# A hybrid decoder layer: the order written out by hand goes on behind attention over ten branch tiles, with the first block sums of h inside it

## The chip, the cores and the metric

The kernel runs on one core of a Trainium2 chip. The metric is the device time of one execution in microseconds, lower is better. Times are medians over several executions. TensorE (PE) does the matmuls, VectorE (DVE) and ScalarE (ACT) the elementwise work and the reading of PSUM, SyncE (SP) issues the DMAs.

## The reference

One layer of width 1024 over 1024 positions in float32 (cut):

```python
h = rms_norm(x, norm_mix_pre)
q, k, v, cb, cc, cx, g_att, g_conv = split(h @ w_in)
y_att  = stick_breaking_attention(heads(q), heads(k), heads(v)) @ w_att_branch
y_conv = (cb * causal_dwconv(cc * cx, conv_mix_w)) @ w_conv_branch
merged = sigmoid(g_att) * y_att + sigmoid(g_conv) * y_conv
x = x + rms_norm(merged @ w_out, norm_mix_post)
h = rms_norm(x, norm_ffn_pre)
a, g = split(causal_dwconv(h @ w_up, conv_ffn_w))
x = x + rms_norm((gelu(g) * a) @ w_down, norm_ffn_post)
```

The attention has 8 heads of 64 and is strictly causal; both branches are 512 wide. The change touches the two branch products (`w_conv_branch`, short wc, and `w_att_branch`, short wa), the gates' weights, and sums of blocks of h.

## The kernel before

Each float32 operand is held as a high and a low half in float16, and every product is three passes: high by high, high by low, low by high. A weight is fetched, its squares are summed on ScalarE (`sumsq`, L57) and over the partitions by a matmul with one column (tile `pr`, L83, from a small cast `rb` on VectorE, L74 or L76). From the sum come a scale and its inverse (L90 to L93), and with the scale ScalarE writes the high half (L100, L199) and VectorE the low half (L101, L204).

**Attention.** It stands under `manual_schedule`: the engines get their rows in the order in which the program writes them. Between the units of attention a generator gives out fill tiles: projections, the conv products, the first gates, and the first four tiles of the conv branch (`branch(0, d)`, named wc0 to wc3). One fill step is three matmuls of 128 by 512. A table `steps` holds what else is issued at which fill step. `plan_weight` enters the stages of a weight there: fetch 56 steps ahead of its use, squares 46, total 40, the pr matmul 26, the high half 24 and the low half 20. `plan_p` does the same for the conv branch's input p, whose four pieces are split four steps apart.

**Behind attention** the order is set by the scheduler of Tile. There stand the conv tiles wc4 to wc7, the attention tiles wa0 to wa5 (24 matmuls each, two halves of 12 with a bank of PSUM each), and the gates. A half is read out with its scale `sgn` by ScalarE (conv, L498) or by VectorE (attention, L500), and its squares are summed on ScalarE. The weights wa0 to wa3 come from `prep`, which fetches and splits them in the order of a fixed sequence; each serves two tiles.

**Block sums.** The gates g1 to g7 are products by a scheme of seven block products in place of eight (`Pair`, `Gates`). It needs sums and differences of blocks of h. `blocks(q)` forms them for the two pairs of 128-row blocks, q = 0 and 1, on VectorE, each row over 128 by 1024: T1 (three rows, L689 to L693), T2 from T1, T4 from T2 (two rows each) and T3 (three rows). `halves` splits each (high on ScalarE, L679, low on VectorE, L680): T1, T2 and T3 into the three parts of hB, T4 over a part of hT. The gate weight has sums of its own (`pair_sums`) and four splits (`pair_split`). The products of a gate (L1093) follow as pg1a, pg1b, pg1c and so on; the pr of the next gate weight, g2, stands between pg1a and pg1b.

Of the kernel before, what the change touches and what calls it, by code (L numbers as in the profile page):

```python
# [38 lines left out]
class Layer:  # L39
# [278 lines left out]
    def mixer(self, mid):  # L318
        tc, nc, a = self.tc, self.nc, self.a
        hT = self.hp.tile([P, 2, KD, T], F16, tag="hT", name="hT")  # L320
        with ExitStack() as ph1:
# [157 lines left out]
            def branch(bi, d, pm):  # L479

                which = ("wc", "wa")[bi]
                name = f"{which}{d // 2}"
                w, inv = self.wdone[name] if bi == 0 else self.prep(name)
                sc = sgn[:, 4 * bi + d // 2:4 * bi + d // 2 + 1]
                if d % 2 == 0:
                    self.mul(sc, inv_x[bi], inv)
                y = self.slot([P, T], F32, f"y{which}{d}")
                for c in range(2):
                    ps = pm.tile([P, NH], F32, tag="pm", name=f"py{which}{d}_{c}")
                    n = 0  # L490
                    for k in range(4):
                        for wi, hi in PASSES:
                            nc.tensor.matmul(ps, w[0][:, wi, ds((d % 2) * NH + k * P, P)],  # L493
                                             acts[bi][k][:, hi, ds(c * NH, NH)], start=n == 0, stop=n == 11)
                            n += 1
                        yield
                    if bi == 0:
                        nc.scalar.activation(y[:, ds(c * NH, NH)], ps, AF.Copy, scale=sc)  # L498
                    else:
                        nc.vector.tensor_scalar(y[:, ds(c * NH, NH)], ps, sc, None, ALU.mult)  # L500
                self.sumsq(y, smy[:, 8 * bi + d:8 * bi + d + 1], f"y{which}{d}")
                ys[which, d] = y
# [105 lines left out]
            steps, n_fill = {}, 0  # L608
            for g, n, names in fill:
# [49 lines left out]
            with tc.manual_schedule(engines=ENGINES):  # L659
# [13 lines left out]
        m16 = []  # L673
        with ExitStack() as ph2:
            hB = self.h7p.tile([P, 2, 3, KH, NH], F16, tag="hB", name="hB")
            t4s = []

            def halves(dst, src):
                nc.scalar.activation(dst[:, 0], src, AF.Copy)  # L679
                nc.vector.tensor_tensor(dst[:, 1], src, dst[:, 0], ALU.subtract)  # L680

            def blocks(q):
                lo, hi = ds(0, NH), ds(NH, NH)
                kA, kB = ds(2 * q, 2), ds(KH + 2 * q, 2)

                def diff(name, p, m, hT_m=True):

                    t = self.slot([P, 2, NH], F32, f"{name}_{q}")
                    nc.vector.tensor_tensor(t, hT[:, 0, p[0], p[1]], hT[:, 0, m[0], m[1]] if hT_m else m,  # L689
                                            ALU.subtract)  # L690
                    nc.vector.tensor_tensor(t, t, hT[:, 1, p[0], p[1]], ALU.add)
                    if hT_m:
                        nc.vector.tensor_tensor(t, t, hT[:, 1, m[0], m[1]], ALU.subtract)  # L693
                    return t
                t1 = diff("T1", (kA, hi), (kA, lo))
                halves(hB[:, :, 0, ds(2 * q, 2), :], t1)
                t2 = diff("T2", (kB, hi), t1, False)
                halves(hB[:, :, 1, ds(2 * q, 2), :], t2)
                t4s.append(diff("T4", (kB, lo), t2, False))
                t3 = diff("T3", (kB, hi), (kA, hi))  # L700
                halves(hB[:, :, 2, ds(2 * q, 2), :], t3)

            def branches(*ds_):
                for d in ds_:
                    for _ in branch(1, d, pm):
                        pass

            def merge_m(d):
                for which, yw in (("gc", "wc"), ("ga", "wa")):
# [4 lines left out]
                return m
# [508 lines left out]
```

## Time and profile before

| | |
|---|---|
| median of 3 runs | 1371.24 us (1370.97 to 1372.31) |
| profiled execution, its own time | 1372.84 us |
| its span | 1371.1 us |
| mean granted clock of TensorE | 0.984 |
| TensorE busy | 1294.1 us, 94% |
| VectorE busy | 1004.2 us, 73% |
| ScalarE busy | 802.0 us, 58% |
| first matmul of wc4 | 406.90 us |
| first matmul of pg1a | 478.21 us |
| first matmul of pg3a | 533.46 us |

The last three rows are read from TensorE's timeline, in microseconds from the span's start. In the profile, L493 is a line of the program, and names are shown without their numbers: pywc is any conv tile, pywa any attention tile, T any of T1 to T4. An idle time is that of an engine just before a row, with what ended it. The granted clock is a share of full speed.

### The profile page before, as it was taken

To read this page: it belongs to the slowest core of one execution; us is meant where nothing else is said; L and a number is where in the kernel's file an instruction comes from. 1 tells how busy PE (TensorE), PEld (TensorE's weight loads), DVE (VectorE), ACT (ScalarE), POOL (GpSimd) and SP (SyncE) were. 2 spreads that over 40 slices of the span, in tenths; PEclk is the share of its full clock that TensorE was granted. 3 is DMA by queue.
4 is the path that set the end of the run, shared out by engine and by line. 5 is a ranking of instruction groups with operands and counts; after the bars stand their busy time and mean duration, and the time that the engine had idled before them with its cause. 6 is when DMAs were issued, how large, how long until landed. Compare 5 with 4: busy or idle time off the path is not lost. (4 is left out here: it accounts for less than half of the span.)

```text
span 1371.1 us, 16955 instructions
## 1 busy us (share of the span) xinstructions
PE 1294.1 (94%) x6543; PEld 592.0 (43%) x6543; DVE 1004.2 (73%) x1649; ACT 802.0 (58%) x1138; POOL 48.1 (4%) x69
## 2 busy tenths in 40 slices
PE   5999999999888789999999999999999999999997
PEld 2444434444333334444444444444444444444443
DVE  5478788787742988877898958945972892698748
ACT  6366565656565365665565666755764764576422
POOL 1000000000000000000110000010001001000001
PEclk9999999999999899999999999999999999999999
DMA  6034444445341112241421143265137228612115
GB/s 262 1 75 100 99 100 101 100 93 108 73 108 32 31 62 77 77 183 33 154 99 51 37 169 138 62 139 145 55 107 156 91 77 208 191 60 95 62 62 199
DMA packets 109392, 139.58 MB, mean 102 GB/s; under 512 B 79088, under 2 KB 79088, under 8 KB 109312
## 3 DMA queue, kind: packets, MB, share of 16 engines
q1 hardware_dynamic: 105360, 124.28, 30.3%
q0 software_dynamic: 3952, 14.23, 5.7%
q8 instruction: 51, 0.84, 0.2%
q14 instruction: 29, 0.24, 0.1%
HBM read 94.45 MB, written 25.17 MB: 87 GB/s over the span
## 5 line engine op out<-in xcount | busy, mean ns | idle before, releaser
L1093 PEld LDWEIGHTS <-wh_u 128*128 128x128 f16 x1848 | 178.8, 98 | 217.9 <-issue 4.1
L988 PE MATMUL pd<-wdh,f 128*128 128x512 f16 x1056 | 235.6, 385 | 10.1 <-DVE wdh L101 5.6
L988 PEld LDWEIGHTS <-f 128*128 128x128 f16 x1056 | 104.5, 99 | 139.8 <-issue 16.4
L1093 PEld LDWEIGHTS <-wh_g 128*128 128x128 f16 x588 | 57.1, 98 | 74.4 <-ACT jk_ywa L57 4.7
L803 PE MATMUL py<-wh_wo,m 128*128 128x512 f16 x384 | 83.9, 379 | 0.0
L100 ACT ACTIVATE wh_u<-ws_u,sc 128x1024 f16<-128x1024 f32 (+1 forms) x66 | 64.2, 998 | 25.6 <-DVE ws_u L928 13.1
L101 DVE SCALAR_TENSOR_TENSOR wh_u<-ws_u,sc,wh_u 128x1024 f16<-128x1024 f32 (+1 forms) x66 | 72.2, 1100 | 7.7 <-ACT wh_u L100 7.7
L992 ACT ACTIVATE y<-pd,sd 128x512 f32<-128x512 f32 x64 | 42.0, 693 | 60.5 <-PE pd L988 54.1
L542 DVE TENSOR_TENSOR_SCAN R<-R,zero 128x256 f32<-128x256 f32 (+3 forms) x64 | 49.2, 811 | 29.0 <-ACT R L529 28.9
L90 DVE TENSOR_SCALAR sc<-pr 128x1 int32<-128x1 int32 x75 | 10.9, 151 | 73.1 <-PE pr L83 73.1
L1170 DVE SCALAR_TENSOR_TENSOR ugu<-cgu,cw_g,ugu 128x1023 f32<-128x1023 f32 (+1 forms) x44 | 56.3, 1279 | 10.3 <-ACT ugu L1168 10.2
L1170 DVE SCALAR_TENSOR_TENSOR ua<-cau,cw_a,ua 128x1023 f32<-128x1023 f32 (+1 forms) x44 | 56.2, 1278 | 1.9 <-ACT ua L1168 1.8
L803 PEld LDWEIGHTS <-m 128*128 128x128 f16 x384 | 37.5, 98 | 44.1
L493 PE MATMUL pywa<-o,wh_wa 128*128 128x512 f16 x192 | 49.1, 420 | 1.9 <-ACT wh_wa L100 1.9
L529 ACT ACTIVATE R<-z,cz 128x1024 f32<-128x1024 f32 (+3 forms) x48 | 42.9, 894 | 13.0 <-PE z L525 8.1
L250 PE MATMUL pcc<-hT,wh_cc 128*128 128x512 f16 x192 | 44.4, 386 | 5.1 <-DVE k L407 5.1
L493 PE MATMUL pywc<-p,wh_wc 128*128 128x512 f16 x192 | 42.8, 379 | 6.4 <-ACT ywc L498 3.8
L354 PE MATMUL pv<-wh_v,hT 128*128 128x512 f16 x192 | 44.4, 382 | 4.0 <-DVE r_pre L217 1.7
L57 ACT ACTIVATE jk_u<-ws_u 128x1024 bf16<-128x1024 f32 x44 | 46.4, 1055 | 2.6 <-DMA ws_u<-w_up_nt 1.9
L561 DVE TENSOR_TENSOR R<-be,R 128x1024 f16<-128x1024 f32 (+3 forms) x48 | 45.3, 944 | 2.3 <-ACT R L559 2.0
L250 PE MATMUL pq<-hT,wh_q 128*128 128x512 f16 x192 | 43.8, 379 | 2.1 <-ACT hT L239 1.2
L551 DVE TENSOR_TENSOR be<-be,R 128x1024 f32<-128x1024 f32 (+3 forms) x48 | 45.7, 952 | 0.1
(610 smaller groups left out, 2523.8 us busy)
## 6 DMA issues: line engine op xcount, KB each, us to landing
ws_u<-w_up_nt SPq DMA_DIRECT2D x44, 512.0 KB, 3.5
yd<-y POOLq DMA_DIRECT2D x24, 512.0 KB, 5.3
ds<-w_down SPq DMA_DIRECT2D x22, 512.0 KB, 6.2
wd<-w_down SPq DMA_DIRECT2D x22, 512.0 KB, 3.5
ws_g<-w_in_nt SPq DMA_DIRECT2D x14, 512.0 KB, 3.5
x<-x SPq DMA_DIRECT2D x8, 512.0 KB, 8.6
ws_wo<-w_out SPq DMA_DIRECT2D x8, 512.0 KB, 6.6
xr<-x SPq DMA_DIRECT2D x8, 512.0 KB, 4.0
```

Source lines behind the costliest of these rows:

```text
L57: self.nc.scalar.activation(self.junk(f"jk_{name}"), src, AF.Square, accum_out=acc)
L100: self.nc.scalar.activation(dst[:, 0, :], src, AF.Copy, scale=s)
L101: self.nc.vector.scalar_tensor_tensor(dst[:, 1, :], src, s, dst[:, 0, :], ALU.mult, ALU.subtract)
L250: nc.tensor.matmul(ps, w[:, wi, ds(k * P, P)], hT[:, hi, k, ds(c * NH, NH)], start=n == 0, stop=n == last)
L493: nc.tensor.matmul(ps, w[0][:, wi, ds((d % 2) * NH + k * P, P)], acts[bi][k][:, hi, ds(c * NH, NH)], start=n == 0, stop=n == 11)
L542: nc.vector.tensor_tensor_scan(rev, rev, self.zero.broadcast_to([P, W]), 2.0 ** 14 if u["top"] else carry[tl][:, h, :], ALU.mult, ALU.add)
L551: nc.vector.tensor_tensor(t["be"][:, :, :W], t["be"][:, :, :W], t["R"][:, :, 1:W + 1], ALU.mult)
L561: nc.vector.tensor_tensor(wv[1], be[:, :, :W], wv[0], ALU.subtract)
L803: nc.tensor.matmul(ps, m16[k][:, hi, ds(tt * P, P)], wo[k][:, wi, sl], start=k == 0 and p == 0, stop=k == 7 and p == 2)
L988: nc.tensor.matmul(ps, f16[g][k][:, hi, ds(tt * P, P)], w[k][:, wi, sl], start=n == 0, stop=n == 3 * GROUPS[g] - 1)
L1093: nc.tensor.matmul(ps, w[wt][:, wi, ds(wc * NH + k * P, P)], self.block(i, hi, k), start=first and n == 0, stop=n == 3 * KH - 1, skip_grou ...
L1170: nc.vector.scalar_tensor_tensor(u[:, lag:], c[:, :T - lag], sm[:, 2 - lag:3 - lag], u[:, lag:], ALU.mult, ALU.add)
```

## The change

The written order goes on over ten more tiles, wc4 to wc7 and wa0 to wa5, at eight fill steps each. In its table now stand: the gate weight g1 with all stages (`plan_pair`, from step 22 of the new stretch on), the block sums T1 and T2 with their halves (`plan_blocks`, from steps 2 and 20 on), the first gating and merging. `plan_weight` now plans wc2, wc3 and wa0 to wa3, 16 steps apart, and `prep` isn't called for them. T3 and T4 come behind the stretch (`late_blocks`), T4 in place in T2's buffer. The first half of an attention tile is read out by ScalarE, the second by VectorE as before. The pieces of p are split three steps apart in place of four. No matmul and no DMA is added or taken away; eight reads of PSUM move from VectorE to ScalarE.

```diff
-                for f, q in [(total, 3), (across, 13), (power, 14)] + [(part(j), 15 + 4 * j) for j in range(4)]:
+                for f, q in [(total, 3), (across, 13), (power, 14)] + [(part(j), 15 + 3 * j) for j in range(4)]:
...
-                w, inv = self.wdone[name] if bi == 0 else self.prep(name)
+                w, inv = self.wdone[name]
...
-                    if bi == 0:
+                    if bi == 0 or c == 0:
                         nc.scalar.activation(y[:, ds(c * NH, NH)], ps, AF.Copy, scale=sc)
...
-            for e in (2, 3):
-                self.plan_weight(steps, f"wc{e}", n_fill + 16 * (e - 2))
+            for e in range(6):
+                self.plan_weight(steps, ("wc2", "wc3", "wa0", "wa1", "wa2", "wa3")[e], n_fill + 16 * e)
...
+            def plan_blocks(steps, q, at):
...
+                for f, g in ((lambda: sub(new("T1"), hT[:, 0, kA, hi_], hT[:, 0, kA, lo_]), 0),
+                             (lambda: add(t["T1"], t["T1"], hT[:, 1, kA, hi_]), 2),
+                             (lambda: sub(t["T1"], t["T1"], hT[:, 1, kA, lo_]), 4),
+                             (lambda: high(b1, t["T1"]), 6),
+                             (lambda: sub(new("T2"), hT[:, 0, kB, hi_], t["T1"]), 6),
+                             (lambda: low(b1, t["T1"]), 8),
+                             (lambda: add(t["T2"], t["T2"], hT[:, 1, kB, hi_]), 10),
+                             (lambda: high(b2, t["T2"]), 12),
+                             (lambda: low(b2, t["T2"]), 14)):
+                    steps.setdefault(at + g, []).append(f)
...
+            def late_blocks(q, t):
...
+                t3, t4 = self.slot([P, 2, NH], F32, f"T3_{q}"), t["T2"]
+                sub(t3, hT[:, 0, kB, hi_], hT[:, 0, kA, hi_])
+                add(t3, t3, hT[:, 1, kB, hi_])
+                sub(t3, t3, hT[:, 1, kA, hi_])
+                b3, b4 = hB[:, :, 2, ds(2 * q, 2), :], hT[:, :, kA, hi_]
+                high(b3, t3)
+                sub(t4, hT[:, 0, kB, lo_], t4)
+                low(b3, t3)
+                add(t4, t4, hT[:, 1, kB, lo_])
+                high(b4, t4)
+                low(b4, t4)
...
+                plan = [(fetch, 0), (lambda: squares(0), 10), (lambda: squares(1), 12), (done, 12), (total, 17),
+                        (lambda: self.pair_sums(n), 22), (across, 30), (power, 31)]
+                plan += [(lambda i=i, e=e: part(i, e), 32 + 4 * i + 3 * e) for i in range(4) for e in range(2)]
...
-            for d in range(4, 8):
-                for _ in branch(0, d, pm):
-                    pass
-            branches(0)
-            ms = [merge_m(0)]
-            branches(1, 2)
-            self.pair_fetch("g1")
...
+            later = [(branch(0, d, pm), 8) for d in range(4, 8)] + [(branch(1, d, pm), 8) for d in range(6)]
+            tq = [plan_blocks(steps, q, n_fill + 2 + 18 * q) for q in range(2)]
+            plan_pair(steps, "g1", n_fill + 22)
+            steps.setdefault(n_fill + 3, []).append(lambda: gated("gc", "wc"))
+            steps.setdefault(n_fill + 45, []).append(lambda: gated("ga", "wa"))
+            steps.setdefault(n_fill + 47, []).append(merged)
+            with tc.manual_schedule(engines=ENGINES):
+                for g, n in later:
+                    for _ in range(n):
+                        for f in steps.pop(state["done"], ()):
+                            f()
+                        next(g)
+                        state["done"] += 1
+                    next(g, None)
+            self.pair_fetch("g2")
             for q in range(2):
-                blocks(q)
-            branches(3)
-            for q in range(2):
-                halves(hT[:, :, ds(2 * q, 2), NH:], t4s[q])
-            self.pair_sums("g1")
-            self.pair_split("g1")
-            self.pair_fetch("g2")
-            branches(4, 5)
+                late_blocks(q, tq[q])
             self.pair_sums("g2")
```

How the rows stand on VectorE behind the last weight split of the conv branch, wh_wc3, before (rb, pr and sc of the sums of wa0 to wa2, wh_wa0 the low half of the first attention weight):

```order
L204 SCALAR_TENSOR_TENSOR wh_wc3_3777<-ws_wc3_3564,sc27_3681,wh_wc3_3777 128x1024
L76 CAST rb29_3986<-sm_wa0_3980 128x1
L90 TENSOR_SCALAR sc28_3985<-pr29_3988 128x1
L92 TENSOR_SCALAR sc28_3985<-sc28_3985 128x1
L93 TENSOR_SCALAR sc28_3985<-sc28_3985 128x1
L104 TENSOR_TENSOR sgn_446<-cst_438,sc28_3985 128x1
L76 CAST rb30_4047<-sm_wa1_3996 128x1
L101 SCALAR_TENSOR_TENSOR wh_wa0_0_3993<-ws_wa0_0_3981,sc28_3985,wh_wa0_0_3993 128x1024
L76 CAST rb31_4058<-sm_wa2_4001 128x1
```

and now, in the same place (T1_0 and T2_0 are the block sums of the first pair):

```order
L680 TENSOR_TENSOR T1_0_3878<-hT_104 128x1024
L794 TENSOR_TENSOR ywc0_3641<-ywc0_3641,sgc0_3361 128x1024
L683 TENSOR_TENSOR T1_0_3878<-T1_0_3878,hT_104 128x1024
L680 TENSOR_TENSOR T1_0_3878<-T1_0_3878,hT_104 128x1024
L90 TENSOR_SCALAR sc28_3784<-pr29_3896 128x1
L92 TENSOR_SCALAR sc28_3784<-sc28_3784 128x1
L93 TENSOR_SCALAR sc28_3784<-sc28_3784 128x1
L76 CAST rb30_3914<-sm_wa1_3787 128x1
L680 TENSOR_TENSOR T2_0_3920<-hT_104,T1_0_3878 128x1024
L680 TENSOR_TENSOR hB_3864<-T1_0_3878,hB_3864 128x1024
L204 SCALAR_TENSOR_TENSOR wh_wa0_3911<-ws_wa0_3685,sc28_3784,wh_wa0_3911 128x1024
L683 TENSOR_TENSOR T2_0_3920<-T2_0_3920,hT_104 128x1024
```

Block rows stand between the small rows of the sums, and the cast of wa0's sum stands ahead of this piece. Further on in the stretch the two rows of T4, written into T2's buffer, stand among them as well, for both pairs.

On TensorE the pr of wa0 (pr29) stood between the last conv tile, wc7, and the first attention tile, and that of wa1 inside it:

```order
L493 MATMUL pywc7_1_3964<-p16_3_3577,wh_wc3_3777 128x512
L83 LDWEIGHTS ones_85
L83 MATMUL pr29_3988<-rb29_3986,ones_85 128x1
L493 LDWEIGHTS wh_wa0_0_3993
L493 MATMUL pywa0_0_4013<-o16_0_993,wh_wa0_0_3993 128x512
```

Now the pr of wa0 stands in the second half of tile wc4:

```order
L493 MATMUL pywc4_1_3889<-p16_1_3509,wh_wc2_3679 128x512
L83 LDWEIGHTS ones_85
L83 MATMUL pr29_3896<-rb29_3785,ones_85 128x1
L493 LDWEIGHTS wh_wc2_3679
L493 MATMUL pywc4_1_3889<-p16_2_3541,wh_wc2_3679 128x512
```

In the same way those of wa1 and wa2 now stand in wc6 and wa0, and those of g1 and wa3 in wa2.

On VectorE ahead of the cast of g2's sum (rb34), which TensorE needs between pg1a and pg1b, stood before the read-out of wa5, one row of T3 and splits of g1:

```order
L500 TENSOR_SCALAR ywa5_4293<-pywa5_0_4294,sgn_446 128x512
L500 TENSOR_SCALAR ywa5_4293<-pywa5_1_4308,sgn_446 128x512
L73 TENSOR_REDUCE sc33_4344<-sm_g2_4252 128x1
L693 TENSOR_TENSOR T3_1_4185<-T3_1_4185,hT_104 128x1024
L928 TENSOR_TENSOR ws_g1_0_4143<-ws_g1_0_4143,s12_g1_4226 128x512
L101 SCALAR_TENSOR_TENSOR wh_g1_1_4240<-ws_g1_1_4147,sc32_4230,wh_g1_1_4240 128x1024
L74 CAST rb34_4345<-sc33_4344 128x1
```

and now:

```order
L500 TENSOR_SCALAR ywa5_4264<-pywa5_1_4279,sgn_446 128x512
L680 TENSOR_TENSOR T3_0_4305<-hT_104 128x1024
L683 TENSOR_TENSOR T3_0_4305<-T3_0_4305,hT_104 128x1024
L680 TENSOR_TENSOR T3_0_4305<-T3_0_4305,hT_104 128x1024
L680 TENSOR_TENSOR hT_104<-T2_0_3920,hT_104 128x2x512
L680 TENSOR_TENSOR T3_1_4315<-hT_104 128x1024
L680 TENSOR_TENSOR hB_3864<-T3_0_4305,hB_3864 128x1024
L683 TENSOR_TENSOR T3_1_4315<-T3_1_4315,hT_104 128x1024
L73 TENSOR_REDUCE sc33_4345<-sm_g2_4296 128x1
L104 TENSOR_TENSOR sc_g1_4417<-g_pre_122,sc31_4087 128x1
L991 TENSOR_TENSOR s12_g2_4325<-ws_g2_1_4301 128x512
L680 TENSOR_TENSOR T3_1_4315<-T3_1_4315,hT_104 128x1024
```

The cast of g2's sum is the row behind the last of these. The whole of T3 and a low half of T4, written to hT, now stand ahead of it, and the splits of g1 are done earlier.

More of the change, by code (lines that the diff above doesn't have):

```diff
@@ L663, in mixer @@
                 attention()
-            self.wpos = self.fpos = len(self.wseq) - 4
             pha.close()
@@ L675, in mixer @@
             hB = self.h7p.tile([P, 2, 3, KH, NH], F16, tag="hB", name="hB")
[L676 to L701, printed above, removed]
@@ new lines, in mixer, with k_of, sub, add @@
+            lo_, hi_ = ds(0, NH), ds(NH, NH)
+            def k_of(q):
+                return ds(2 * q, 2), ds(KH + 2 * q, 2)
+            def sub(out, x, y):
+                nc.vector.tensor_tensor(out, x, y, ALU.subtract)
+            def add(out, x, y):
+                nc.vector.tensor_tensor(out, x, y, ALU.add)
+            def high(dst, src):
+                nc.scalar.activation(dst[:, 0], src, AF.Copy)
+            def low(dst, src):
+                sub(dst[:, 1], src, dst[:, 0])
+            def plan_blocks(steps, q, at):
+                kA, kB = k_of(q)
+                t = {}
+                b1, b2 = [hB[:, :, e, ds(2 * q, 2), :] for e in range(2)]
+                def new(name):
+                    t[name] = self.slot([P, 2, NH], F32, f"{name}_{q}")
+                    return t[name]
+                for f, g in ((lambda: sub(new("T1"), hT[:, 0, kA, hi_], hT[:, 0, kA, lo_]), 0),
[8 more added lines that the diff above has]
+                    steps.setdefault(at + g, []).append(f)
+                return t
@@ new lines, in late_blocks @@
+            def late_blocks(q, t):
+                kA, kB = k_of(q)
+                t3, t4 = self.slot([P, 2, NH], F32, f"T3_{q}"), t["T2"]
[9 more added lines that the diff above has]
+                low(b4, t4)
@@ new lines, in plan_pair, with fetch, squares, done @@
+            def plan_pair(steps, n, at):
+                h = {}
+                def fetch():
+                    h["sm"] = self.small(f"sm_{n}", w=8)
+                    h["t"] = [self.ws.tile([P, D], F32, tag="ws", name=f"ws_{n}_{i}") for i in range(2)]
+                    for t, src in zip(h["t"], self.psrc[n]):
+                        nc.sync.dma_start(t, src)
+                def squares(i):
+                    self.sumsq(h["t"][i], h["sm"][:, i:i + 1], f"{n}_{i}")
+                def done():
+                    self.praw[n] = h["sm"], h["t"]
+                def total():
+                    h["r"] = self.scale_sum(h["sm"], 2)
+                def across():
+                    h["r"] = self.scale_mm(*h["r"])
+                def power():
+                    h["s"], h["inv"] = self.scale_pow(*h["r"], 1)
+                    h["w"] = [self.wh.tile([P, 2, D], F16, tag="wh", name=f"wh_{n}_{i}") for i in range(4)]
+                    self.pw[n] = h["w"], h["inv"]
+                def part(i, e):
+                    ua, ug, s12 = self.praw[n][1:]
+                    src = (ua, ug, s12, ua[:, hi_])[i]
+                    w = h["w"][i] if i < 3 else h["w"][3][:, :, :NH]
+                    if e == 0:
+                        nc.scalar.activation(w[:, 0], src, AF.Copy, scale=h["s"])
+                    else:
+                        nc.vector.scalar_tensor_tensor(w[:, 1], src, h["s"], w[:, 0], ALU.mult, ALU.subtract)
+                        if i == 0:
+                            sub(ua[:, hi_], ua[:, hi_], s12[:, hi_])
+                plan = [(fetch, 0), (lambda: squares(0), 10), (lambda: squares(1), 12), (done, 12), (total, 17),
+                        (lambda: self.pair_sums(n), 22), (across, 30), (power, 31)]
+                plan += [(lambda i=i, e=e: part(i, e), 32 + 4 * i + 3 * e) for i in range(4) for e in range(2)]
+                for f, g in plan:
+                    steps.setdefault(at + g, []).append(f)
@@ L720, in split_m, with gated, merged @@
                 m16.append(t)
-            for d in range(4, 8):
-                for _ in branch(0, d, pm):
-                    pass
-            branches(0)
-            ms = [merge_m(0)]
-            branches(1, 2)
-            self.pair_fetch("g1")
-            self.inv_h = inv_h
-            for q in range(2):
-                blocks(q)
-            branches(3)
-            for q in range(2):
-                halves(hT[:, :, ds(2 * q, 2), NH:], t4s[q])
-            self.pair_sums("g1")
-            self.pair_split("g1")
-            self.pair_fetch("g2")
-            branches(4, 5)
+            self.inv_h = inv_h
+            ms = []
+            def gated(which, yw):
+                y = ys[yw, 0]
+                nc.vector.tensor_tensor(y, y, sig[which, 0], ALU.mult)
+            def merged():
+                add(ys["wa", 0], ys["wa", 0], ys["wc", 0])
+                ms.append(ys["wa", 0])
+            later = [(branch(0, d, pm), 8) for d in range(4, 8)] + [(branch(1, d, pm), 8) for d in range(6)]
[12 more added lines that the diff above has]
+                    next(g, None)
+            assert not steps, sorted(steps)
+            self.pair_fetch("g2")
+            for q in range(2):
+                late_blocks(q, tq[q])
             self.pair_sums("g2")
```

## The prediction

> **What bounds the kernel now.** I read the busy times first, then a table of windows around the branch products, then TensorE's timeline there, the waits, and the lines that fill VectorE and ScalarE. The page's first part:
>
> ```profile
> PE 1294.1 (94%) x6543; PEld 592.0 (43%) x6543; DVE 1004.2 (73%) x1649; ACT 802.0 (58%) x1138; POOL 48.1 (4%) x69
> ```
>
> TensorE is the bound of the whole, so only its idle time and its slow clock can be won. Where they lie, by windows (start and end, length, busy time and count of PE, weight loads, DVE, ACT, POOL, then the granted clock, the DMA share and GB/s):
>
> ```profile
> 370.00:407.00 37.00, 30.27 (x193) 14.54 (x192) 20.62 (x34) 23.05 (x32) 0.00 (x0) 1.00 0.43 106
> 407.00:428.00 21.00, 20.78 (x96) 9.30 (x95) 0.00 (x0) 9.47 (x16) 0.00 (x0) 1.00 0.02 9
> 428.00:479.00 51.00, 36.85 (x153) 15.76 (x153) 42.81 (x64) 24.37 (x34) 0.00 (x0) 0.83 0.14 42
> 479.00:534.00 55.00, 49.81 (x220) 21.80 (x218) 44.52 (x72) 31.93 (x48) 0.00 (x0) 0.94 0.18 58
> 534.00:620.00 86.00, 86.00 (x405) 39.06 (x403) 70.18 (x117) 57.57 (x85) 1.13 (x2) 1.00 0.36 123
> ```
>
> From 407 to 428 (tiles wc4 to wc7) PE is full and VectorE does nothing at all for 21 us. From 428 to 479 VectorE is busy 42.81 of 51 us and PE waits for 14. After 534 PE is busy all the time, so what is won before is kept there. TensorE's timeline (start, duration, what, idle before and releaser):
>
> ```profile
> 382.96 0.16 PE L83 MATMUL pr<-rb,ones 128*128 128x1 bf16 x1 [0.32 <-ACT sga L477]
> 387.48 4.04 PE L493 MATMUL pywc<-p,wh_wc 128*128 128x512 f16 x18 [3.05 <-ACT ywc L498]
> 406.90 20.88 PE L493 MATMUL pywc<-p,wh_wc 128*128 128x512 f16 x96 [0.78 <-ACT ywc L498]
> 431.11 0.16 PE L83 MATMUL pr<-rb,ones 128*128 128x1 bf16 x1 [3.33 <-DVE rb L76]
> 433.14 1.89 PE L493 MATMUL pywa<-o,wh_wa 128*128 128x512 f16 x4 [1.87 <-ACT wh_wa L100]
> 464.99 0.16 PE L83 MATMUL pr<-rb,ones 128*128 128x1 bf16 x1 [9.17 <-DVE rb L74]
> 481.65 2.75 PE L1093 MATMUL pg1a<-hT,wh_g 128*128 128x512 f16 x12 [0.69 <-ACT cgg L1108]
> 488.81 0.16 PE L83 MATMUL pr<-rb,ones 128*128 128x1 bf16 x1 [4.41 <-DVE rb L74]
> 533.46 2.75 PE L1093 MATMUL pg3a<-hT,wh_g 128*128 128x512 f16 x12
> ```
>
> Every long stop stands ahead of a pr: the one-column matmul that sums a weight's squares over the partitions. It waits for the cast rb on VectorE; the waits of 428 to 515 add up to:
>
> ```profile
> DVE rb L76 <- ACT jk_wa L57: 26.4, 2, 26.2
> PE pr L83 <- DVE rb L74: 13.6, 2, 9.2
> PE pr L83 <- DVE rb L76: 3.3, 1, 3.3
> ```
>
> The first row is VectorE's empty time: its next row, the sum of wa0, waited 26.2 us for squares that came late. The block sums, which need only hT and were ready long before, stand behind it. The 9.17 us are the second effect: the sum of g1 stands on VectorE among the block sums. And a stop costs more than itself; the clock after two of them, and around 390 after the 3.05 us:
>
> ```profile
> 387.00:390.00 3.00, 2.52 (x12) 1.17 (x12) 1.55 (x6) 1.45 (x3) 0.00 (x0) 1.00 0.83 155
> 465.00:468.00 3.00, 3.00 (x9) 1.07 (x9) 3.00 (x4) 1.82 (x2) 0.00 (x0) 0.50 0.00 0
> 468.00:471.00 3.00, 3.00 (x9) 1.11 (x8) 3.00 (x6) 0.52 (x2) 0.00 (x0) 0.53 0.00 0
> 489.00:492.00 3.00, 3.00 (x8) 1.06 (x7) 3.00 (x3) 0.43 (x1) 0.00 (x0) 0.50 0.47 175
> 492.00:495.00 3.00, 3.00 (x9) 1.06 (x8) 2.94 (x9) 2.44 (x4) 0.00 (x0) 0.55 0.32 66
> ```
>
> A matmul takes 20.88 / 96 = 0.2175 us at full clock, so 6 us hold 27.6; after 9.17 us idle they held 18 and after 4.41 us 17. Such a stop costs 2.1 to 2.3 us beside itself; 3.05 us idle cost none.
>
> **The budget.** From 406.90 (first matmul of wc4) to 488.81 (pr of g2, between pg1a and pg1b) pass 81.9 us. They hold ten branch tiles and pg1a, 264 matmuls or 57.4 us at full clock; 3.33 + 1.87 + 9.17 + 0.69 + 4.41 = 19.5 us idle; and 5.0 us left over, which is the halved clock after the stops at 431 and 465 and the small rows.
>
> **The change part by part.** PE's work and order of tiles stay; ten tiles of 24 matmuls take 52.2 us, so without a stop wa5 ends at 406.9 + 52.2 = 459.1 in the clock of this trace (478.21 before, where pg1a begins). Whether it does depends on the hand-offs, which I walked through on all engines with these durations (the last number ahead of the bar is the count, the second behind it the mean in ns):
>
> ```profile
> L691 DVE TENSOR_TENSOR T<-T,hT 128x1024 f32<-128x1024 f32 x8 | 9.5, 1220 | 0.1
> L101 DVE SCALAR_TENSOR_TENSOR wh_wa<-ws_wa,sc,wh_wa 128x1024 f16<-128x1024 f32 x4 | 5.1, 1281 | 1.8 <-ACT wh_wa L100 1.8
> L500 DVE TENSOR_SCALAR ywa<-pywa,sgn 128x512 f32<-128x512 f32 x16 | 11.6, 744 | 2.4 <-PE pr L83 1.4 <-PE pywa L493 1.0
> L913 DVE TENSOR_TENSOR s_g<-ws_g 128x512 f32<-128x512 f32 x4 | 2.7, 681 | 0.0
> L498 ACT ACTIVATE ywc<-pywc,sgn 128x512 f32<-128x512 f32 x8 | 5.5, 687 | 11.4 <-PE pywc L493 11.4
> L57 ACT ACTIVATE jk_ywa<-ywa 128x1024 bf16<-128x1024 f32 x8 | 8.4, 1055 | 20.5 <-DVE ywa L500 16.1 <-DVE sc L90 4.4
> L679 ACT ACTIVATE hB<-T 128x1024 f16<-128x1024 f32 x6 | 6.3, 1049 | 3.7 <-DVE T L693 2.4 <-DVE T L691 1.2
> ```
>
> *Block sums and g1 ahead of wa.* VectorE is free from 404.7 (end of the last wc split, at 403.41 with 1.28). Up to the cast of g1's sum its new order holds 18 block rows and the gate of ywc0 at 1.22, two splits at 1.28 and 12 tiny rows at about 0.15: 27.6 us, which ends at 432.3 without gaps. Low parts wait for ScalarE's high parts of 1.05 us, and the scales of wa0 and wa1 for their pr; my walk puts 5.9 us for that, so the cast ends at 438.2. TensorE needs it after 156 matmuls, at 406.9 + 33.9 = 440.8: 2.6 us of room. For wa3 the walk gives 439.4 against 442.1, for the weights themselves 418.8 against 427.8 (wa0), 430.9 against 438.2 (wa1), 442.7 against 448.6 (wa2). In all, VectorE has 43 to 47 us of work in the 54.3 from 404.7 to 459, ScalarE about 41 in 51. So these moves cost nothing and take away the stops at 431, 433 and 465. Without that cover each pr costs its lateness one to one, and about 2.2 more once a stop passes some 3.5 us.
>
> *First halves evicted on ScalarE.* Eight rows of 0.744 us leave VectorE, eight of about 0.687 come to ScalarE. ScalarE is the emptier (9.47 of 21 us and 24.37 of 51); the cost is order: at the end of wa5 its row of pg1a (cgg) stands behind jk_ywa4, two rows of wa5 and the high part of T4. That puts it at 464.25, so the second half of pg1a starts 2.65 us late (0.69 before).
>
> *The block sums that stay late.* After wa5's last matmul VectorE must still do, ahead of g2's cast: the eviction (0.74), the three rows of T3 of the first pair, the low part into hT, a row of T3, the low part into hB, two more rows of T3 (8 x 1.22 = 9.76), one half sum of g2 (0.68) and three tiny rows (0.45). That is 11.6 us, and 0.4 for ScalarE's high part in between: 459.1 + 12.0 = 471.1. PE is done with pg1a at 464.25 + 2.75 = 467.0, so g2's pr stops it for 4.1 us. The pair pg1a and pr is thus as badly placed as before, only earlier: 471.1 for 488.81, a gain of **17.7 us**. Check by the budget: 57.4 + 2.65 + 4.1 = 64.2, 17.7 under 81.9.
>
> From there to pg3a it took 533.46 - 488.81 = 44.65 us, with the half clock of 489 to 495 in it. A stop of 4.1 follows too, so I leave that as it is, and the same holds for the weights of g2, whose DMA is fetched earlier by as much.
>
> *Closer splits of p, and wc2, wc3, wa0 planned in the table.* The stop at 387.48 hangs on VectorE's sgn, released late:
>
> ```profile
> 379.41 1.28 DVE L101 SCALAR_TENSOR_TENSOR p<-pf,sc,p 128x1024 f16<-128x1024 f32 x1 [2.70 <-ACT p L100]
> 380.61 1.28 DVE L204 SCALAR_TENSOR_TENSOR wh_wc<-ws_wc,sc,wh_wc 128x1024 f16<-128x1024 f32 x1
> 386.50 0.15 DVE L104 TENSOR_TENSOR sgn<-sc,sc 128x1 f32<-128x1 f32 x1
> 386.75 0.69 ACT L498 ACTIVATE ywc<-pywc,sgn 128x512 f32<-128x512 f32 x1 [2.81 <-DVE sgn L104]
> ```
>
> With the last part of p (1.28) ahead of it in a gap of 2.70, sgn comes about 1.2 us sooner and pywc at 387.48 with it. Against that, wa0's squares (1.05) and its 512 KB on SP now stand in the attention's tail, among the transposes: at worst the whole 1.2 is lost and 1.0 more. I take 1.2, since both engines idle there.
>
> **Sum.** 17.7 + 1.2 = 18.9 of the profiled execution's 1372.84: 1353.9. The median of the runs shown is 1371.24, 1.6 lower: **1352.3 us**.
>
> **A rule against the row.** The clock fell after idle of 4.41 us and not after 3.05. The Trainium skill, page "TensorE: Matmul & The Clock Gate", section "Part 1: The HAM clock gate (the "warmup" mystery)", gives a free-running window of about 3.4 us, and half clock until some 3.4 us of work have gone by. By that a stop costs 1.7 us in place of the 2.1 to 2.3 that the rows show, an estimate from its figure. As the window is free-running, a stop of 4.1 us need not fill one: by the page the time is the forecast or 1.7 less, 1350.6, depending on where the window falls, which no trace here shows.
>
> **The rivals.**
> *VectorE stays the limit, and the stops come back smaller (0.23).* For it: rooms of 2.6 and 2.7 us under 5.9 us of hand-offs that I could only estimate; the low parts pay a round trip through ScalarE each. If every one of some 25 crossings takes 0.3 us more than I gave it, 7.5 in all, the sums of g1 and wa3 come about 5 us after they are needed, with one stop at half clock on top: 5 + 2.2 = 7.2 less gain, about 1359. Against it: 428 to 479 shows VectorE keeping 42.81 of 51 us.
> *The last stop is not punished, or shorter (0.11).* If ScalarE reaches cgg in time, or T3 is put earlier by the engines' slack, the two stops shrink: 2.3 us of clock and up to 2.65 of pg1a: 1347 to 1349.
> *Slower (0.05).* Sums standing inside tiles hold matmuls that could run: PE takes its rows in order. If wa1, g1 and wa3 each wait as long as the two of L74 did (13.6 / 2 = 6.8, and 2.2 for the clock: 9 each, 27 together), the gain of 18.9 turns to 8 lost, 1379. It decides from a sum of 18.9 us of new stops on. Against it: each row of squares stands at least 18 fill steps of three matmuls (54 x 0.2175 = 11.7 us) ahead of its pr.
> *The gain is given back (0.03).* A transfer of g2 or g3 arrives no sooner than before and pg3a starts at 533 again: 1371. Fetches take 3.5 us and queues are nearly idle (0.14 and 0.18 in the windows):
>
> ```profile
> ws_g<-w_in_nt SPq DMA_DIRECT2D x14, 512.0 KB, 3.5
> ```
>
> **How the numbers follow.** The forecast has 0.58 and its own range, 1349.5 to 1355.5: the tail's term between -1.0 and 1.2, the late chain by one row of 1.22, the clock. The range is 1346 to 1360: the second rival whole and most of the first. A measurement of this kernel tells 0.2% (2.7 us) from no change. Faster: 0.58 + 0.23 + 0.11 = 0.92; same 0.03; slower 0.05.
>
> **What would show it.** VectorE is no longer empty while wc4 to wc7 run; the ten tiles take 52 to 53 us; no pr before pg1a waits over 1 us; a stop of about 4 us stays ahead of the pr between pg1a and pg1b, with about half clock behind it, and one of about 2.6 inside pg1a; the stop after pywc's first half is near 2 us in place of 3.05; after pg3a the two traces run alike. I am wrong if a pr inside wc4 to wa3 waits 3 us or more, or if the matmuls of the wa tiles run spread out.

## The result and the profile after

The changed kernel takes 1350.49 us (median, 1349.2 to 1353.69) against 1371.78 for the kernel before measured beside it: the ratio is 0.9843, 95% interval 0.9818 to 0.9868, so 1.6% or 21.3 us faster. The forecast was 1352.3 in a range of 1346 to 1360. The profiled execution took 1349.20 us.

TensorE's timeline of the changed kernel (start, duration, what, idle before and releaser):

```profile
382.92 0.16 PE L83 MATMUL pr<-rb,ones 128*128 128x1 bf16 x1 [1.43 <-ACT sga L477]
385.99 4.04 PE L493 MATMUL pywc<-p,wh_wc 128*128 128x512 f16 x18 [1.59 <-ACT ywc L498]
405.40 4.04 PE L493 MATMUL pywc<-p,wh_wc 128*128 128x512 f16 x18 [0.78 <-ACT ywc L498]
409.29 0.17 PE L83 MATMUL pr<-rb,ones 128*128 128x1 bf16 x1
419.67 0.17 PE L83 MATMUL pr<-rb,ones 128*128 128x1 bf16 x1
430.06 0.17 PE L83 MATMUL pr<-rb,ones 128*128 128x1 bf16 x1
439.15 0.17 PE L83 MATMUL pr<-rb,ones 128*128 128x1 bf16 x1
440.47 0.17 PE L83 MATMUL pr<-rb,ones 128*128 128x1 bf16 x1
457.33 2.75 PE L1171 MATMUL pg1a<-hT,wh_g 128*128 128x512 f16 x12
461.57 2.75 PE L1171 MATMUL pg1a<-hT,wh_g 128*128 128x512 f16 x12 [1.49 <-ACT cgg L1186]
468.78 0.16 PE L83 MATMUL pr<-rb,ones 128*128 128x1 bf16 x1 [4.46 <-DVE rb L74]
468.80 5.28 PE L1171 MATMUL pg1b<-hB,wh_g 128*128 128x512 f16 x12
513.17 2.75 PE L1171 MATMUL pg3a<-hT,wh_g 128*128 128x512 f16 x12
```

No pr between 405 and 457 has an idle time ahead of it any more, and the one between pg1a and pg1b has kept its own. By stage, from such rows of both kernels:

| stage | before, us | forecast, us | after, us |
|---|---|---|---|
| start to wc4 | 406.90 | 405.7 | 405.40 |
| wc4 to pg1a, the ten tiles | 71.31 | 52.2 | 51.93 |
| pg1a to the pr of g2 | 10.60 | 12.0 | 11.45 |
| that pr to pg3a | 44.65 | 44.65 | 44.39 |
| pg3a to the end of the profiled execution | 839.38 | 839.4 | 836.03 |

The ten tiles give 19.4 us, and up to pg3a the gain is 20.29 us in these two traces (18.9 forecast). The last row's 3.35 us is no part of the change. Behind pg3a the clock of the kernel before falls to half three times amid the work (at 798.5, 1126.1 and 1320.7 us), that of the changed kernel once (at 709.6), each time for 3.4 us, which costs about 1.7, so that two falls fewer make up the 3.35. In the twelve traces below this piece takes 833.97 to 838.93 us. The first row scatters as well: a second trace of the changed kernel reaches wc4 at 408.11 us. What the change did there is read from the stop, 3.05 us before and 1.59 after.

The windows of the changed kernel (columns as in the prediction):

```profile
402.00:428.00 26.00, 25.22 (x120) 11.36 (x118) 19.63 (x26) 17.52 (x26) 0.00 (x0) 1.00 0.14 42
428.00:459.00 31.00, 31.00 (x148) 14.07 (x146) 25.19 (x41) 21.32 (x34) 0.00 (x0) 1.00 0.25 82
459.00:469.00 10.00, 4.05 (x20) 1.69 (x18) 9.79 (x13) 9.67 (x16) 0.00 (x0) 0.92 0.03 10
469.00:513.20 44.20, 44.10 (x195) 19.39 (x194) 30.39 (x51) 20.83 (x29) 0.00 (x0) 0.94 0.16 48
```

VectorE, empty from 407 to 428 before, is now busy for 19.63 of the 26 us from 402 to 428, with TensorE at full clock. From 459 to 469 both VectorE and ScalarE are full and TensorE is not: that is where the block sums that stayed late stand. VectorE's rows at the places with the least room:

```profile
436.28 0.16 DVE L74 CAST rb<-sc 128x1 bf16<-128x1 f32 x1
437.32 0.15 DVE L76 CAST rb<-sm_wa 128x1 bf16<-128x1 f32 x1
439.41 1.28 DVE L204 SCALAR_TENSOR_TENSOR wh_wa<-ws_wa,sc,wh_wa 128x1024 f16<-128x1024 f32 x1 [1.94 <-ACT wh_wa L199]
457.53 0.75 DVE L500 TENSOR_SCALAR ywa<-pywa,sgn 128x512 f32<-128x512 f32 x1 [0.44 <-PE pywa L493]
468.57 0.15 DVE L74 CAST rb<-sc 128x1 bf16<-128x1 f32 x1
```

The cast of g1's sum ended at 436.44 and was needed at 439.15, a room of 2.7 us (2.6 forecast); that of wa3 had 3.0 (2.7 forecast). From the last read-out of wa5 to the cast of g2's sum VectorE took 11.2 us.

### The profile page after: what moved, and what is told of

Its sections match the earlier page's. It is cut to its first block, busy times and chain, and to the rows that moved or that the text cites. A ratio compares the mean times of both kernels' runs of the same rounds, so it can differ in the third digit from the quotient of the medians.

```text
span 1347.4 us, 16966 instructions
## 1 busy us (share of the span) xinstructions
PE 1285.3 (95%) x6543; PEld 589.8 (44%) x6543; DVE 1000.6 (74%) x1641; ACT 806.1 (60%) x1146; POOL 48.1 (4%) x69
## 5 line engine op out<-in xcount | busy, mean ns | idle before, releaser
L1066 PE MATMUL pd<-wdh,f 128*128 128x512 f16 x1056 | 230.5, 379 | 10.4 <-DVE wdh L101 5.8
L1171 PEld LDWEIGHTS <-wh_g 128*128 128x128 f16 x588 | 57.5, 99 | 77.0 <-issue 10.4
L1246 ACT ACTIVATE ua<-cau,cw_a 128x1024 f32<-128x1024 f32 x22 | 25.1, 1140 | 33.8 <-DVE cau L1198 31.4
```

Of the source, the lines that this page charges most:

```text
L1066: nc.tensor.matmul(ps, f16[g][k][:, hi, ds(tt * P, P)], w[k][:, wi, sl], start=n == 0, stop=n == 3 * GROUPS[g] - 1)
L1171: nc.tensor.matmul(ps, w[wt][:, wi, ds(wc * NH + k * P, P)], self.block(i, hi, k), start=first and n == 0, stop=n == 3 * KH - 1, skip_grou ...
```

## The experiments

Differences of one or two microseconds are read from the traces, as the time from wc4 to pg1a and from pg1a to pg3a; the medians scatter by about as much. The changed kernel run again took 1351.15 us (ratio 0.9844, 0.9830 to 0.9857), and where a median below is set against the changed kernel, it is this one. It had 51.92 and 55.54 us in these two stages.

> The changed kernel again, as a reference for the others on the same chip: 1350 to 1351 us, 21 under the kernel before.

### The pieces of p four steps apart again

```diff
-    ... [(part(j), 15 + 3 * j) for j in range(4)]:
+    ... [(part(j), 15 + 4 * j) for j in range(4)]:
```

> The pieces of p are split four steps apart again, all else as changed. If the closer spacing is what brought sgn and the second half of tile wc2's read-out forward (the stop at 385.99 was 1.59 us after the change, 3.05 before), that stop is back near 3.05 and the time is 1.2 to 1.5 us above the changed kernel. If another part of the change did it (the weights planned in the table), the time stays and the stop stays near 1.6.

It took 1353.19 us (ratio 0.9860, 0.9847 to 0.9874), 2.0 above the changed kernel. TensorE's row behind the stop, and two windows there, with the border where the clock falls:

```profile
387.42 5.73 PE L493 MATMUL pywc<-p,wh_wc 128*128 128x512 f16 x18 [3.05 <-ACT ywc L498]
```

```profile
384.89:388.30 3.41, 0.88 (x5) 0.41 (x5) 1.69 (x3) 1.62 (x2) 0.00 (x0) 1.00 0.55 104
388.30:391.72 3.42, 3.42 (x10) 1.18 (x9) 2.38 (x7) 1.84 (x4) 0.00 (x0) 0.50 0.56 107
```

The stop is back at 3.05 us: the closer spacing alone took 1.46 us off it. And here the same 3.05 us that were followed by full clock in the kernel before (18 matmuls in 4.04 us) were followed by half clock: 5.73 us, 1.69 more.

### The first halves of the wa tiles read out by VectorE

```diff
-                    if bi == 0 or c == 0:
+                    if bi == 0:
```

> VectorE reads out the first halves of the wa tiles again, all else as changed. VectorE sat idle for about 12 of the 52 us of the ten tiles, so six reads of 0.74 us cost PE nothing there: no pr inside the tiles waits over 0.5 us. And since the scheduler then puts the cast of g2's sum ahead of three of the late block rows (about 3.7 us), and the read-out of pg1a no longer waits behind two reads on ScalarE, the stops before pg1b shrink from 1.49 + 4.46 to about 1.5 in all: 3 to 6 us faster than the changed kernel. Rival: moving these reads is what gives VectorE the room; then the sums of g1 and wa3 stop PE inside tile wa2 and the time is 3 to 5 us above the changed kernel.

It took 1347.22 us (ratio 0.9812, 0.9798 to 0.9825), 3.9 below the changed kernel. No pr inside the tiles waited; the two late stops:

```profile
461.85 2.75 PE L1171 MATMUL pg1a<-hT,wh_g 128*128 128x512 f16 x12 [0.68 <-ACT cgg L1186]
467.51 0.16 PE L83 MATMUL pr<-rb,ones 128*128 128x1 bf16 x1 [2.91 <-DVE rb L74]
467.53 4.44 PE L1171 MATMUL pg1b<-hB,wh_g 128*128 128x512 f16 x12
```

Together 3.59 us in place of 5.95, and less half clock; pg1a to pg3a took 52.56 us in place of 55.84. As forecast, the cast of g2's sum stands behind five block rows in place of eight. I had expected 1.5 us of stops; VectorE now starts T3 only behind three read-outs of wa4 and wa5. VectorE had room for these reads, and moving them changed the order at the end for the worse.

### The block sums T1 and T2 behind the tiles, the rest as changed

```diff
-            tq = [plan_blocks(steps, q, n_fill + 2 + 18 * q) for q in range(2)]
...
             for q in range(2):
-                late_blocks(q, tq[q])
+                own = {}
+                t = plan_blocks(own, q, 0)
+                for g in sorted(own):
+                    for f in own[g]:
+                        f()
+                late_blocks(q, t)
```

> As changed, but the block sums T1 and T2 with their halves stand behind the ten tiles, beside T3 and T4; the written order and the planned weights stay. If the block sums in VectorE's empty time are what the gain rests on, half of it or more goes: the cast of g2's sum comes about 2 us later (10 rows of 1.22 us ahead of it in place of eight and small ones), and pg1b and pg1c then wait for low parts of T1 and T2 of the second pair, 4 to 8 us more, with half clock behind a stop: 1359 to 1366. Rival: the gain is that the weights of wa and g1 are planned ahead, and the block sums could stand anywhere: at most 1353.

It took 1352.57 us (ratio 0.9873, 0.9856 to 0.9889). That is 1.4 above the changed kernel. The tiles still took 51.92 us; pg1a to pg3a took 59.15 in place of 55.84. The rival's number came, not mine. TensorE's two longest stops, then the windows of the tiles and of the stretch behind:

```profile
461.59 2.75 PE L1175 MATMUL pg1a<-hT,wh_g 128*128 128x512 f16 x12 [2.10 <-ACT cgg L1190]
468.27 0.16 PE L83 MATMUL pr<-rb,ones 128*128 128x1 bf16 x1 [3.93 <-DVE sc L73]
```

```profile
404.80:456.70 51.90, 51.89 (x245) 23.59 (x245) 22.89 (x46) 33.72 (x52) 0.00 (x0) 1.00 0.20 66
468.30:515.90 47.60, 44.42 (x196) 19.34 (x196) 47.47 (x67) 27.18 (x37) 0.00 (x0) 0.95 0.14 45
```

With only two block rows in them (at 452.42 and 453.67 us, behind the last sum of the tiles), the tiles run as well as with all of T1 and T2. The late rows fill VectorE to 47.47 of 47.60 us, but TensorE has the last wa tiles and g2's first products to do meanwhile, so that only about 3.3 us show in the trace. The gain of the tiles is that of the sums; the early block rows keep part of it from being given back.

### The kernel before with wa0 alone planned

```diff
+            self.plan_weight(steps, "wa0", n_fill + 19)
...
-            self.wpos = self.fpos = len(self.wseq) - 4
+            self.wpos = self.fpos = len(self.wseq) - 3
```

> The kernel before, with wa0 alone planned in the table (19 steps behind the end of the fill, so that its sum and split are done inside attention). The 26.2 us for which VectorE waited for wa0's squares are gone, and with them the stops of 3.33 and 1.87 us and the half clock behind them (about 2). If the late place of the block sums is the second cause, the stop ahead of g1's pr stays (9.17 us in the kernel before; 7 to 10 here), and the gain is 6 to 8 us: 1363 to 1366. Rival: the wait for wa0's squares alone held everything up, and most of the gain comes: 1356 or less. Other rival: the stop only grows at the next pr: over 1369.

It took 1365.21 us (ratio 0.9962, 0.9947 to 0.9977), 5.4 less than the kernel before. TensorE:

```profile
429.08 5.34 PE L493 MATMUL pywa<-o,wh_wa 128*128 128x512 f16 x24
460.94 0.16 PE L83 MATMUL pr<-rb,ones 128*128 128x1 bf16 x1 [10.28 <-DVE rb L74]
```

The tile wa0 starts without a stop, and g1's pr waits 10.28 us in place of 9.17. Two causes, then, and the second is untouched by the first.

### The kernel before with all block sums moved behind the tiles; then with wa0 planned too

```diff
-            for q in range(2):
-                blocks(q)
             branches(3)
-            for q in range(2):
-                halves(hT[:, :, ds(2 * q, 2), NH:], t4s[q])
...
             branches(4, 5)
+            for q in range(2):
+                blocks(q)
+            for q in range(2):
+                halves(hT[:, :, ds(2 * q, 2), NH:], t4s[q])
```

> The kernel before, with all block sums moved behind the ten tiles and nothing else changed: the scheduler then puts the cast of g1's sum behind no block row. If the 9.17 us stop of g1's pr came from the block rows between g1's squares and its cast, it falls under 2 us and the half clock behind it goes, while the stops of wa0 stay (3.33 and 1.87 us) and the late block rows add 3 to 6 us ahead of pg1b and pg2: 1361 to 1366. Rival: g1's weights come too late by themselves (fetch or squares), and the stop stays over 5 us: 1370 or more.

> The same with wa0 planned in the table as well, still in the scheduler's own order. If the stops of wa0 and of g1's sum are two causes that add up, and the written order matters only through them: 1370.6 less 5.4 (wa0 alone) less 11 (g1's stop and its clock) plus 3 to 6 for the late block rows: 1356 to 1361. Rival: the written order gains by itself, and without it less than half of the 21 us comes: 1362 or more.

The first took 1368.21 us (ratio 0.9972, 0.9960 to 0.9985), the second 1360.82 (0.9909, 0.9882 to 0.9936). TensorE in the first, and then in the second:

```profile
433.19 0.16 PE L83 MATMUL pr<-rb,ones 128*128 128x1 bf16 x1 [3.33 <-DVE rb L76]
459.51 0.16 PE L83 MATMUL pr<-rb,ones 128*128 128x1 bf16 x1 [0.97 <-DVE rb L74]
478.59 0.38 PE L1093 MATMUL pg1b<-hB,wh_g 128*128 128x512 f16 x1 [2.26 <-ACT hB L679]
```

```profile
453.01 0.16 PE L83 MATMUL pr<-rb,ones 128*128 128x1 bf16 x1 [1.64 <-DVE rb L74]
```

With no block row ahead of it, g1's sum is late by 0.97 us in place of 9.17: the block rows were the stop. By stage:

| kernel | wc4 to pg1a, us | pg1a to pg3a, us |
|---|---|---|
| before | 71.31 | 55.25 |
| wa0 planned | 65.63 | 55.25 |
| block sums behind the tiles | 60.91 | 61.28 |
| both of these | 54.32 | 61.60 |
| changed, T1 and T2 behind the tiles | 51.92 | 59.15 |
| changed | 51.93 | 55.84 |

In the first column the two causes add up, nearly: 5.7 and 10.4 alone, 17.0 together of the 19.4. The second column shows the price of late block rows: 6 us in the scheduler's order, which is why the first of these two kernels came 2 us above its expected range, and 3.3 in the written one.

### More rows on VectorE ahead of g1's sum

Rows whose result is used by nothing stand ahead of the cast, four in the first kernel, two in the second:

```diff
+            def load():
+                nc.vector.tensor_tensor(self.extra, hT[:, 0, k_of(0)[1], lo_], hT[:, 0, k_of(1)[1], lo_], ALU.subtract)
+            self.extra = self.slot([P, 2, NH], F32, "extra")
+            for n in range(4):
+                steps.setdefault(n_fill + 38, []).insert(0, load)
```

> As changed, with four more rows of 128 by 1024 on VectorE (4.9 us) ahead of the cast of g1's sum; their result is used by nothing, and the output is the same. The cast ended 2.7 us ahead of its pr, as forecast (2.6). If that room is what separates the change from a stop, the pr of g1 stops PE by about 2.2 us and the time is 2 to 3 us above the changed kernel. If VectorE had all the slack that its 12 us of idle time in the ten tiles suggest: 0 to 0.5. If VectorE is the limit of the stretch: 4.5 or more.

> As changed, with two rows of 128 by 1024 on VectorE (2.45 us) ahead of the cast of g1's sum (four of them stopped g1's pr by 1.85 us, and moved the pr of g2 back by 4.1 us). If VectorE and ScalarE run from there to g2's cast as one chain of hand-offs whose idle times come back unchanged however late it is, no pr inside the tiles waits (2.45 is under the room of 2.7), yet the pr of g2 comes 2.0 to 2.5 us later, and the time rises by 1.5 to 2.5 us. Rival: the idle times of VectorE behind that place (1.94, 1.34, 0.63, 0.44 us) take the rows up: pr of g2 within 0.5 us of where it was, no change.

With four rows: 1353.69 us (ratio 0.9877, 0.9863 to 0.9892), and wc4 to pg3a 110.97 us in place of 107.77, so 3.2 more. With two: 1352.55 us (0.9852, 0.9829 to 0.9876), 108.72, so 1.0 more. TensorE with four rows, then with two:

```profile
441.13 0.18 PE L83 MATMUL pr<-rb,ones 128*128 128x1 bf16 x1 [1.85 <-DVE rb L74]
466.20 4.44 PE L1177 MATMUL pg1a<-hT,wh_g 128*128 128x512 f16 x12 [4.13 <-ACT cgg L1192]
472.88 0.16 PE L83 MATMUL pr<-rb,ones 128*128 128x1 bf16 x1 [2.23 <-DVE rb L74]
472.90 4.44 PE L1177 MATMUL pg1b<-hB,wh_g 128*128 128x512 f16 x12
```

```profile
461.07 2.75 PE L1177 MATMUL pg1a<-hT,wh_g 128*128 128x512 f16 x12 [1.51 <-ACT cgg L1192]
469.87 0.16 PE L83 MATMUL pr<-rb,ones 128*128 128x1 bf16 x1 [6.05 <-DVE rb L74]
```

VectorE's wait behind g1's cast, in the kernel with two rows:

```profile
441.04 1.28 DVE L204 SCALAR_TENSOR_TENSOR wh_wa<-ws_wa,sc,wh_wa 128x1024 f16<-128x1024 f32 x1 [1.94 <-ACT wh_wa L199]
```

The room at g1's pr is as read: 4.9 us of rows make a stop of 1.85, 2.45 us none. But the late pr of g2 moves back in both, since VectorE's chain to it takes up little. With two rows, g1's cast and the row shown come 2.1 us later than in the changed kernel, counted from the first matmul of wc4, and the wait for ScalarE's high half of wa2's weight is 1.94 us as it was. Idle time of this kind is a hand-off and no slack. Only the wait of 0.44 us for TensorE, ahead of wa5's last read-out, is used up. So the stop at g2's pr grew by 1.6 us, where I had expected 2.0 to 2.5, and 0.6 of that came back as clock: half clock ended 4.0 us behind this pr in place of 5.3. In the medians 1.4 us are left of an expected 1.5 to 2.5.

### The written order over the start of g1

The order goes on past the tiles: g1's products 1, 6 and 5 (pg1a's first half, pg1b, pg1c) come first, the sum of g2 behind T3 of the first pair, T4 later. T4's two sums get steps of their own in the table, and so do the fetch and the squares of g2's first half.

```diff
+                fetch2(1)
+                gp[1].prod(1)
+                next(g, None)
+                t3 = third(0)
+                self.sumsq(g2["t"][1], g2["sm"][:, 1:2], "g2_1")
+                r2 = self.scale_sum(g2["sm"], 2)
+                low(hB[:, :, 2, ds(0, 2), :], t3)
+                gp[1].prod(6)
+                gp[1].prod(5)
+                high(hT[:, :, k_of(0)[0], hi_], tq[0]["T2"])
+                low(hT[:, :, k_of(0)[0], hi_], tq[0]["T2"])
+                self.s_of["g2"] = self.scale_pow(*self.scale_mm(*r2), 1)
+                t3 = third(1)
...
```

> As changed, but the written order goes on over the start of g1: PE does pg1a's first half, then pg1b and pg1c (which need only T1 and T2), then pg1a's second half, then the pr of g2; the cast of g2's sum stands behind three block rows of T3 in place of eight rows, and T4's high part behind pg1a's read-out. If what is left of the cost is the two stops before pg1b (1.49 and 4.46 us) and the half clock behind them (about 2.2), they are gone and nothing takes their place: 6 to 8 us under the changed kernel, 1342 to 1345, with the clock at full from 457 on. Rival: the late block sums are the limit, and the stop only moves to the products that need T3, or to the first product of g2 whose weights come later: 0 to 3 us under it.

It took 1340.51 us (1338.35 to 1342.0; ratio 0.9766, 0.9753 to 0.9780), 10.6 below the changed kernel and 2.3% below the kernel before. TensorE's timeline, then its windows:

```profile
458.19 2.75 PE L1194 MATMUL pg1a<-hT,wh_g 128*128 128x512 f16 x12
460.78 2.75 PE L1194 MATMUL pg1b<-hB,wh_g 128*128 128x512 f16 x12
463.37 2.75 PE L1194 MATMUL pg1c<-hB,wh_g 128*128 128x512 f16 x12
465.96 2.75 PE L1194 MATMUL pg1a<-hT,wh_g 128*128 128x512 f16 x12
468.55 0.17 PE L83 MATMUL pr<-rb,ones 128*128 128x1 bf16 x1
```

```profile
458.00:469.00 11.00, 11.00 (x53) 5.00 (x52) 7.37 (x13) 9.99 (x18) 0.00 (x0) 1.00 0.15 51
469.00:505.00 36.00, 36.00 (x170) 16.41 (x169) 33.95 (x54) 23.35 (x33) 0.00 (x0) 1.00 0.18 59
```

Both stops and the half clock are gone, and nothing has taken their place: pg1a to pg3a took 46.70 us, 9.1 less than in the changed kernel (6 to 8 expected). The kernel moves several things at once, and no run takes them apart. That the early block sums pay here, because pg1b and pg1c need only T1 and T2, is argued and not shown.

Two kernels more on this one, the two extra rows and the reads moved back to VectorE:

> The written order over the start of g1, with the same two rows on VectorE. There g2's pr was not waited for, and stands 11.2 us behind the last matmul of wa5. The two rows then cost nothing: same time as without them (1340.5), no stop over 0.5 us from 405 to 500. Rival: VectorE is the limit there too: 2 us more.

> The written order over the start of g1, with the first halves of the wa tiles read out by VectorE. Moving these reads gained 3.9 us in the changed kernel. If that came from the place of g2's cast and of pg1a's read-out alone, nothing is left to gain here: within 1.5 us of 1340.5. Rival: the reads are slower or in the way on ScalarE itself: 3 to 4 us faster than 1340.5. Other rival: VectorE now lacks the room: a stop at the pr of g1 or wa3, 2 us or more slower.

They took 1340.56 us (ratio 0.9772, 0.9755 to 0.9789) and 1342.72 us (0.9785, 0.9765 to 0.9806). The rows cost nothing in the median, as expected, but 1.0 us in the trace (wc4 to pg3a 99.67 us for 98.62, with one stop of 0.68 at pg2b, where none over 0.5 was expected). The reads, worth 3.9 us in the changed kernel, now cost about 2 (100.50 us in the trace, with stops of 0.52, 0.62 and 0.24 at pg2b), a little more than I expected, and none of it at a pr of the tiles. So what they were worth lay in the order at the end.

## Why the prediction was right, point by point

**What bounds.** Right: only TensorE's idle time and clock were to be won, and the stretch from 407 to 489 held them. From pg3a on the two kernels differ only in where the clock falls.

**The ten tiles without a stop.** Right: 51.93 us for 52.2. The walk through the hand-offs gave the rooms of the sums of g1 and wa3 to within 0.3 us of what was measured, and that carried the forecast. In part this was luck. From 403.11 to the end of g1's cast at 436.44 VectorE was busy for 25.80 us and waited for 7.5, where the walk had 27.6 and 5.9: rows of 1.22 us start as little as 1.13 us apart, so they overlap, and the waits were longer. The two errors cancel.

**What causes the stops.** The prediction named two causes, late squares of wa0 and block rows ahead of g1's sum. Both are shown, each by its own kernel: 5.7 and 10.4 us. It did not say that the early place of the block sums is not needed to remove them; I took that place for the larger part when I set the expected range of 1359 to 1366, and that was wrong. In the tiles it is enough that no block row stands ahead of a sum. Their early place is worth 3.3 us, behind the tiles.

**First halves on ScalarE.** The weakest step: with the reads on VectorE the kernel is 3.9 us faster, 3.3 in the trace. I had read the cost rightly as one of order, but priced only ScalarE's side, the late read-out of pg1a (a stop of 2.65 us forecast, 1.49 measured). I had not seen that with the reads on VectorE the scheduler puts fewer block rows ahead of g2's cast.

**The late chain.** Right in place, 12.0 us forecast, from wa5's last matmul to g2's pr, against 11.45 from the first of pg1a. The two stops in it are off in opposite directions, 1.49 us for 2.65 and 4.46 for 4.1.

**The tail of attention.** 1.2 forecast; the stop shrank by 1.46, and the spacing of p's pieces is shown to be the cause. One sign does not hold as written: the pr at 382.92, in this tail, waits 1.43 us for ScalarE (0.32 before), though it starts no later than before (382.96).

**The clock.** Half right. That a stop of about 4 us would be followed by half clock held, in the changed kernel's windows:

```profile
463.88:467.29 3.41, 0.44 (x3) 0.10 (x1) 3.41 (x6) 3.37 (x6) 0.00 (x0) 1.00 0.00 0
467.29:470.71 3.42, 1.93 (x6) 0.73 (x6) 3.42 (x7) 2.17 (x4) 0.00 (x0) 0.50 0.00 0
470.71:474.12 3.41, 3.41 (x9) 1.21 (x8) 1.79 (x7) 1.64 (x2) 0.00 (x0) 0.50 0.00 0
```

The price of 2.1 to 2.3 us was too low. Two neighbouring windows both count the matmul on their border: cut as one window of 6 us, 465 to 471 and 489 to 495 hold 16 each and not 18 and 17, and the first and last lie only partly in it. The row behind the 9.17 us stop of the kernel before, and one of as many matmuls at full clock in the changed kernel, give 2.8:

```profile
465.01 13.36 PE L493 MATMUL pywa<-o,wh_wa 128*128 128x512 f16 x48
409.31 10.52 PE L493 MATMUL pywc<-p,wh_wc 128*128 128x512 f16 x48
```

The sum did not use that price, since it took the 44.65 us behind the stop over whole; the rivals did. That 3.05 us cost no clock did not hold, as the last section tells.

**The rivals.** No sum inside a tile became a stop, and nothing was given back behind pg3a. Of the second rival a part came: the stop inside pg1a was 1.16 us shorter than forecast, but the one ahead of g2's pr was neither shorter nor spared half clock. The 1350.6 given for a stop that does not bring half clock lies next to the 1350.49 measured, but the half clock came, so this is chance.

## What to carry to other kernels

A short row that another engine waits for, such as the cast of a sum, stands in its queue behind whatever was written ahead of it. Look for the long rows between what it needs and itself; here moving these, to either side, took the stop away. Then follow the first product behind the stretch and ask which of the moved rows it truly needs: here pg1b and pg1c needed two block sums of four, and the order that puts the other work behind them gave half as much again (10.6 us on 21.3).

## What the runs showed that I had not expected

The same stop of 3.05 us, at the same place behind the read-out of tile wc2's half, was followed by full clock in the kernel before (18 matmuls in 4.04 us) and in the one with wa0 planned and the block sums moved (12 in 2.75), and by half clock in three others (18 in 5.73 us in the kernel with p's pieces four steps apart, in the one with wa0 planned, and in the one with the block sums moved). Stops of 2.91 and 2.23 us were followed by a group of 12 matmuls that took 4.44 us in place of 2.75. So the length of a stop alone doesn't decide, and I had taken 3.05 for safe from one trace. Each such case cost 1.69 us; the longer stop of the changed kernel cost about 2.7 (5.28 us for 2.75 in the first group behind it, 2.88 in the next).

What separates the cases is how the stop lies on a grid. In every trace here the granted clock changes only at steps of 3.41 us, at another offset from the span's start in each. In the kernel before it falls at 429.8, 460.6, 487.9, 798.5, 1126.1 and 1320.7 us, which lie 9, 8, 91, 96 and 57 such steps apart. The prediction said that no trace shows where the window falls; this one does. Two steps of that trace, around the stop of 3.05 us:

```profile
385.44:388.85 3.41, 1.37 (x7) 0.65 (x7) 1.65 (x4) 1.63 (x2) 0.00 (x0) 1.00 0.71 133
388.85:392.26 3.41, 3.41 (x31) 1.81 (x31) 2.42 (x7) 2.30 (x3) 0.00 (x0) 1.00 0.56 107
```

Here the first step still held 1.37 us of work, since the stop began ahead of it, and the clock stayed. With p's pieces four steps apart, the step from 384.89 held 0.88 us, and the clock fell at its end, 0.9 us after the work had begun again. In all fourteen traces, from 20 us on, the clock never fell at the end of a step with more than 1.51 us of work and never held after one with less than 1.37.

The Trainium skill, page "TensorE: Matmul & The Clock Gate", section "Part 1: The HAM clock gate (the "warmup" mystery)", says that the window runs freely and lasts about 3.4 us, and that half clock ends after about as much work. The grid of 3.41 us agrees with that, and the 1.69 us with half of it. It puts the fall behind an idle window; here one with 0.88 us of work was followed by half clock too.
